# A two-layer hybrid decoder trunk on one core: the mix chunks spilled from the gate tile through another queue, the weight preparation tied to matmuls, and the second GLA norm emitted inside the first convolution

## The chip, the cores and the metric

The kernel runs on one core of one Trainium2 chip. Its time is the device time of one execution in microseconds (us); the figure quoted is the median of several runs. The engines are named as the profile names them: PE is TensorE (matmuls; PEld are its weight loads), DVE is VectorE, ACT is ScalarE, POOL is GpSimd and SP is SyncE. Each engine works through its own instructions in order. DMAs are issued by an engine's queue: SP's (SPq), ACT's (ACTq) or POOL's (POOLq).

## What is computed

There are two layers over 512 tokens of width 2048 in float32. A layer normalises its input and projects it with one wide matrix. The result feeds three branches, which are joined, projected once more and added to the input:

```python
def _layer(x, norm_g, w_in, conv_w, conv_b, sb_qn_g, sb_kn_g, gla_w_up, gla_b_up, gla_on_g, w_out):
    h = _rmsnorm(x, norm_g)
    cv_h, cv_b, cv_c, cv_g, sb_q, sb_k, sb_v, sb_g, gl_q, gl_k, gl_v, gl_g, gl_lr = split(h @ w_in)
    y_conv = _short_conv(cv_h, cv_b, cv_c, conv_w, conv_b) * silu(cv_g)      # causal, width 3
    y_sb = _stick_breaking(rms(sb_q), rms(sb_k), sb_v) * silu(sb_g)          # 8 heads of 128
    g = log_sigmoid(gl_lr @ gla_w_up + gla_b_up) / 16
    o = _gla(gl_q, gl_k, gl_v, g)                                            # 4 heads, state of 64 x 128
    y_gla = _rmsnorm(o, gla_on_g) * silu(gl_g)
    return x + concatenate([y_conv, y_sb, y_gla], axis=-1) @ w_out
```

So each of the three branches is 512, 1024 and 512 columns of the joined "mix" of 2048 columns, and each is multiplied by a gate of its own.

## The kernel before

**Weights.** Both weight matrices are streamed in groups of 256 columns; a list (`specs`) gives their order. In a layer the groups are: GLA v 0 and v 1 (v 1 with the low-rank columns), GLA q, GLA k, GLA gate 0 and 1, convolution h, c, g, b (half 0), then four times v, g, q, k of the attention, convolution h, c, g, b (half 1), and eight groups of the output matrix. A matmul works in float16 and keeps float32 accuracy by splitting each operand into a high and a low part, with three matmuls for each product. Preparing group i is this chain:

- `fetch` (L359): two DMAs of 1 MB into the staging tile "st", of which there are two. All but the first three groups are issued by POOL.
- `wmax` (L370): a square with an accumulated maximum or sum on ACT, one for each of the two halves of the tile. `wscale` takes the sum over partitions (POOL `partition_all_reduce`, L383) and forms the scale with small DVE instructions.
- then `whi` (ACT, L436) and `wlo` (DVE, L444) write the high and low parts of each half. For the groups called "quick" (the attention's g and k, the convolution's h of half 1, and three or four output groups of a layer) `wsums` writes seven combinations instead (ACT L476, DVE L477, and the accumulating copy L494 on POOL), so that the projection takes seven products rather than eight.

`weights()` is called by each projection for its group i: it starts the fetch of i + 2 and, before this change, `load(i + 1)`: squares, scale and parts of the next group, with high priority and the squares held behind the first high part of group i (`anchor`). The order of the engines' instructions is decided by a scheduler from the order of emission, the dependencies, and these holds (`order` is a dependency without a semaphore's data).

**Projections.** `project_cols` (L663 to L673 are its three matmuls and those of `project_toks`), `project_quick` (L750 and L753) and `project_by_token` (L797) multiply the input's parts with a group's parts into PSUM banks "psp" (three buffers). The quick products are combined by evictions on ACT (L761, L765, L768) and DVE (L763), and TensorE reuses a bank only after its eviction.

**GLA.** The two halves p = 0, 1 run one after the other. For each the level matrices are built (L995 to L1090), the final products (L1090, 48 matmuls) accumulate the half's outputs in PSUM, and for each of two heads hh the norm follows: o times a scale (DVE), its square (ACT L1098), a matmul by `avg` into "psm" (L1100), logarithm and exponential (ACT L1102, L1103), DVE steps L1104 to L1109, of which the last multiplies by the gate `gg[p]`, and `mixsplit`.

**The mix.** `mixsplit` makes the high (ACT L857) and low (DVE L858) parts of one 128-column chunk of the mix in a tile "ga" (two buffers, 128 x 2 x 512 float16) and spills it to DRAM (`mixd`, 256 KB) with a DMA from SP (L860), 24 times in all. The gate tiles have tag "g", two buffers too. `project_gate` (L822 to L829) evicts a gate's projection with ACT (L822) into a "g" tile, then computes its SiLU with four ACT instructions into a "ga" tile (L824 to L826, L828). At half 1 of the convolution `mixload` reads the chunks back.

**Where the stages stand.** The norm of p = 0 runs at the end of convolution half 0, about when its gate is evicted (the first layer's last part of it ends at 237.29 us). The norm of p = 1 is emitted after its final products, ahead of convolution h. In the order of the scheduler these products stand inside the projection of the attention's v 0, and the norm's two matmuls L1100 behind it, ahead of the accumulating products of g 0.

Of the kernel before, what the change touches and what calls it, by code (L numbers as in the profile page):

```python
# [43 lines left out]
def hybrid_trunk(ctx, tc, x, norm_g, w_in, conv_w, conv_b, sb_qn_g, sb_kn_g,  # L44
# [294 lines left out]
    def load(i):  # L339
        with tc.high_priority():  # L340
            load_(i)

# [23 lines left out]
    def wmax(i, h):  # L366

        if h == 0:
            peak[i] = sm(2 + (i in narrow), "wm")
        S.activation(junk(HK * GW).rearrange("p (k n) -> p k n", k=HK), staged[i][h], AF.Square,  # L370
                     accum_out=peak[i][:, h:h + 1])
        if h and i in narrow:
            S.activation(junk(KT * LR).rearrange("p (k n) -> p k n", k=KT), narrow[i], AF.Square,
                         accum_out=peak[i][:, 2:3])

    def wscale(i):
# [4 lines left out]
        if i:  # L381
# [4 lines left out]
            V.tensor_tensor(m, gm[:, 0:1], gm[:, 1:2], ALU.add)  # L386
        else:

            ps = bank(psm, "m")[:, :1]
            pk = peak.pop(i)  # L390
            for j, (a, b) in enumerate(((ones, pk[:, 0:1]), (ones, pk[:, 1:2]), (pk[:, 2:3], pk[:, 2:3]))):
                T.matmul(ps, a.to_broadcast([P, P]), b, start=j == 0, stop=j == 2)
# [10 lines left out]
        scales[i] = sc  # L403

# [26 lines left out]
    anchor = {}  # L431

    def whi(i, h):
# [3 lines left out]
        anchor.setdefault(i, hi)  # L437
# [23 lines left out]

    def wsums(i):
# [18 lines left out]
        if specs[i][1] is w_out:  # L481
# [6 lines left out]
            anchor[i] = split(b12, 2)  # L488
# [7 lines left out]
        anchor[i] = split(b22, 3)  # L496
# [9 lines left out]
    def weights():  # L506
# [140 lines left out]
    for l in range(depth):  # L647
# [3 lines left out]
        def project_cols():  # L651
# [3 lines left out]
            for h in range(2):  # L655
                wh, wl = w[h]
                for c, o in enumerate(ps):
                    cs = slice(c * P, (c + 1) * P)
                    for kk in range(HK):
# [5 lines left out]
                        T.matmul(o, wl[:, kk, cs], xh[:, :, k, :], start=False, stop=en)  # L665
            return ps, u

        def tok_mm(o, ah, al, w, t, k, n, st_, en):
# [4 lines left out]
            T.matmul(o, al[:, t, k, :], wh[:, kk, :n], start=False, stop=en, skip_group_check=True)  # L673

        def project_toks(ah, al, late=()):
# [59 lines left out]
        def project_quick(src, sums, y, cols):  # L735
# [7 lines left out]
            def prod(o, w, a, start, stop=False):  # L743
                for t in range(1 if cols else 2):
                    for kk in range(HK):
                        for i, (p_, q_) in enumerate(((0, 0), (0, 1), (1, 0))):
                            st_ = start and t == kk == i == 0
                            en = stop and kk == HK - 1 and i == 2
                            if cols:
                                T.matmul(o, w[q_][:, kk, :], a[p_][:, :, kk, :], start=st_, stop=en,  # L750
                                         skip_group_check=True)
                            else:
                                T.matmul(o[:, t * P:(t + 1) * P], a[p_][:, t, kk, :], w[q_][:, kk, :], start=st_,  # L753
                                         stop=en, skip_group_check=True)
# [653 lines left out]
```

## Time and profile before

| | us |
|---|---|
| median of 3 runs | 1780.85 |
| lowest, highest | 1779.24, 1786.48 |
| the profiled execution | 1789.68 |
| its span, first to last instruction | 1787.5 |

The granted TensorE clock over the span is 0.981 of full. Busy times in the span: PE 1685.7 us (94%), DVE 1340.1 (75%), ACT 1131.2 (63%), POOL 218.2 (12%). The DMA engines moved 227.25 MB.

A line of the profile gives the line of the kernel, the engine and the operation with its tiles (output, then inputs). A bracket behind an instruction is the time in which its engine stood idle before it and what ended that.

### The profile page before, as it was taken

To read this page: it belongs to the slowest core of one execution; us is meant where nothing else is said; L and a number is where in the kernel's file an instruction comes from. 1 tells how busy PE (TensorE), PEld (TensorE's weight loads), DVE (VectorE), ACT (ScalarE), POOL (GpSimd) and SP (SyncE) were. 2 spreads that over 40 slices of the span, in tenths; PEclk is the share of its full clock that TensorE was granted. 3 is DMA by queue.
4 is the path that set the end of the run, shared out by engine and by line. 5 is a ranking of instruction groups with operands and counts; after the bars stand their busy time and mean duration, and the time that the engine had idled before them with its cause. 6 is when DMAs were issued, how large, how long until landed. Compare 5 with 4: busy or idle time off the path is not lost.

```text
span 1787.5 us, 36869 instructions
## 1 busy us (share of the span) xinstructions
PE 1685.7 (94%) x15642; PEld 1306.6 (73%) x15642; DVE 1340.1 (75%) x2327; ACT 1131.2 (63%) x1619; POOL 218.2 (12%) x262
## 2 busy tenths in 40 slices
PE   7999995999999999999989999959999899999999
PEld 5644554888989884689976454649888888748898
DVE  8966887577777787686688577866777777768874
ACT  7667664576666676566665675556676666755652
POOL 1210110011111111011111101001111111100100
PEclk9999998999999999999999999989999999999999
DMA  7233341357656867355544233224576677763441
GB/s 241 92 98 95 95 118 55 76 131 136 143 136 143 143 166 206 77 163 169 192 98 142 90 100 106 60 59 111 110 170 103 138 134 165 223 150 102 158 144 49
DMA packets 204517, 227.25 MB, mean 127 GB/s; under 512 B 118770, under 2 KB 166204, under 8 KB 203840
## 3 DMA queue, kind: packets, MB, share of 16 engines
q0 software_dynamic: 58432, 162.54, 32.6%
q1 hardware_dynamic: 136912, 52.90, 14.4%
q10 hardware_dynamic: 9008, 9.45, 1.6%
q8 instruction: 122, 2.00, 0.5%
q14 instruction: 43, 0.35, 0.1%
HBM read 179.65 MB, written 14.68 MB: 109 GB/s over the span
## 4 chain that ended last, share of the span: by engine, by line
PE 19%; DVE 13%; DMA 12%; ACT 7%; issue 3%; POOL 1%; POOLq 0%; ACTq 0%; DVEq 0%
DMA st<-in_w_in_dram 5%; PE psp L753 5%; ACT junk L370 3%; DMA st<-in_w_out_dram 3%; PE psp L797 3%; DVE wl L477 3%; DMA qT<-qp 2%; PE psp L673 2%; PE psp L750 2%; PE psp L671 2%; PE psp L672 2%; PE psp L664 1%; PE psp L663 1%; PE psp L665 1%; DVE wl L444 1%
## 5 line engine op out<-in xcount | busy, mean ns | idle before, releaser
L370 ACT ACTIVATE junk<-st 128x2048 uint8<-128x2048 f32 x150 | 285.8, 1905 | 129.6 <-DMA st<-in_w_in_dram 94.9
L444 DVE SCALAR_TENSOR_TENSOR wl<-st,ws,wh 128x2048 f16<-128x2048 f32 x102 | 239.2, 2346 | 51.6 <-ACT wh L436 51.1
L671 PE MATMUL psp<-wh,m 128*128 128x256 f16 x960 | 261.8, 273 | 1.6 <-ACT m L1127 1.6
L672 PE MATMUL psp<-wl,m 128*128 128x256 f16 x960 | 261.8, 273 | 0.0
L673 PE MATMUL psp<-wh,m 128*128 128x256 f16 x960 | 261.8, 273 | 0.0
L436 ACT ACTIVATE wh<-st,ws 128x2048 f16<-128x2048 f32 x100 | 199.1, 1996 | 68.0 <-PE psp L664 32.2
L477 DVE SCALAR_TENSOR_TENSOR wl<-st,ws,wh 128x1024 f16<-128x1024 f32 x150 | 189.4, 1278 | 35.7 <-ACT wh L476 35.6
L476 ACT ACTIVATE wh<-st,ws 128x1024 f16<-128x1024 f32 x150 | 165.6, 1139 | 64.5 <-PE psp L673 33.6
L359 POOL DMA_DIRECT2D st<-in_w_in_dram x114 | 103.7, 926 | 476.9 <-DVE wl L444 219.8
L673 PE MATMUL psp<-wh,x 128*128 128x256 f16 x512 | 139.7, 273 | 0.0
L672 PE MATMUL psp<-wl,x 128*128 128x256 f16 x512 | 139.6, 273 | 0.0
L671 PE MATMUL psp<-wh,x 128*128 128x256 f16 x512 | 139.5, 273 | 0.0
L383 POOL PARTITION_ALL_REDUCE wgm<-wm x75 | 38.1, 508 | 811.1 <-ACT junk L370 797.7
L665 PE MATMUL psp<-x,wl 128*128 128x512 f16 x352 | 134.1, 381 | 2.2 <-DVE wl L444 2.2
L750 PE MATMUL psp<-s,wh 128*128 128x256 f16 x640 | 113.8, 279 | 23.6 <-ACT g L761 21.4
L663 PE MATMUL psp<-x,wh 128*128 128x512 f16 x352 | 134.2, 381 | 0.0
L664 PE MATMUL psp<-x,wh 128*128 128x512 f16 x352 | 133.9, 381 | 0.0
L663 PE MATMUL psp<-m,wh 128*128 128x512 f16 x352 | 133.4, 379 | 0.0
L664 PE MATMUL psp<-m,wh 128*128 128x512 f16 x352 | 133.4, 379 | 0.0
L665 PE MATMUL psp<-m,wl 128*128 128x512 f16 x352 | 133.2, 379 | 0.0
L665 PEld LDWEIGHTS <-wl 128*128 128x128 f16 x704 | 69.0, 98 | 83.2 <-DVE wl L444 2.7
L663 PEld LDWEIGHTS <-wh 128*128 128x128 f16 x704 | 69.0, 98 | 81.4 <-issue 1.7
(426 smaller groups left out, 4001.5 us busy)
## 6 DMA issues: line engine op xcount, KB each, us to landing
st<-in_w_in_dram POOLq DMA_DIRECT2D x114, 1024.0 KB, 8.3
st<-in_w_out_dram POOLq DMA_DIRECT2D x32, 1024.0 KB, 7.6
st<-st POOLq DMA_DIRECT2D x18, 512.0 KB, 9.5
st<-in_w_in_dram SPq DMA_DIRECT2D x6, 1024.0 KB, 11.8
mixd<-ga SPq DMA_DIRECT2D x24, 256.0 KB, 10.0
x<-in_x_dram SPq DMA_DIRECT2D x4, 1024.0 KB, 4.9
qT<-in_x_dram ACTq DMA_DIRECT2D x8, 512.0 KB, 4.7
qT<-xs ACTq DMA_DIRECT2D x8, 512.0 KB, 4.1
```

The costliest lines, as they stand in the source:

```text
L370: S.activation(junk(HK * GW).rearrange("p (k n) -> p k n", k=HK), staged[i][h], AF.Square, accum_out=peak[i][:, h:h + 1])
L436: hi = S.activation(wh[:, :, :GW], staged[i][h], AF.Copy, scale=scales[i])
L444: V.scalar_tensor_tensor(wl[:, :, :GW], staged[i][h], scales[i], wh[:, :, :GW], ALU.mult, ALU.subtract)
L476: hi = S.activation(h_, b, AF.Copy, scale=sc)
L477: V.scalar_tensor_tensor(l_, b, sc, h_, ALU.mult, ALU.subtract)
L663: T.matmul(o, wh[:, kk, cs], xh[:, :, k, :], start=st_, stop=False)
L664: T.matmul(o, wh[:, kk, cs], xl[:, :, k, :], start=False, stop=False)
L665: T.matmul(o, wl[:, kk, cs], xh[:, :, k, :], start=False, stop=en)
L671: T.matmul(o, ah[:, t, k, :], wh[:, kk, :n], start=st_, stop=False, skip_group_check=True)
L672: T.matmul(o, ah[:, t, k, :], wl[:, kk, :n], start=False, stop=False, skip_group_check=True)
L673: T.matmul(o, al[:, t, k, :], wh[:, kk, :n], start=False, stop=en, skip_group_check=True)
L750: T.matmul(o, w[q_][:, kk, :], a[p_][:, :, kk, :], start=st_, stop=en, skip_group_check=True)
```

## The change

There are five edits.

1. `mixsplit` gets the dead half of the gate tile (the half whose gate has just been multiplied in) and writes both parts of the chunk into it, as float16 in the space of 512 float32 numbers a partition. No "ga" tile is taken for this. The spill is issued by POOL instead of SP.
2. `load` and `anchor` are gone. `weights()` leaves two closures in `hooks`; the projection that uses group i calls `hook(mm)` at two of its matmuls. The first hook emits the squares of group i + 1 and orders the first square behind that matmul (the first triple of the projection), the second emits the scale and the parts and orders the first instruction of the scale behind its matmul, which stands about a quarter into the projection. In `project_quick` these are the first triple of the first product and the last matmul of the second product.
3. The norm of GLA's half p becomes a closure for each hh. The first half's are called at once, as before. The second half's are kept and called from the two `then()` points of `conv_in(0)`: after the eviction of convolution h's projection, and after the convolution.
4. `insums = xsums()` (the combined parts of the input for the quick products) is emitted after the loop over GLA's q and k instead of before.
5. The callers of `mixsplit` pass the dead gate half.

The core of the diff:

```diff
-    def load(i):
-        with tc.high_priority():
-            load_(i)
...
 def wmax(i, h):
...
-        S.activation(junk(HK * GW).rearrange("p (k n) -> p k n", k=HK), staged[i][h], AF.Square,
-                     accum_out=peak[i][:, h:h + 1])
+        sq = S.activation(junk(HK * GW).rearrange("p (k n) -> p k n", k=HK), staged[i][h], AF.Square,
+                          accum_out=peak[i][:, h:h + 1])
...
+        return sq
...
 def wscale(i):
...
+        first = V.tensor_tensor(m, gm[:, 0:1], gm[:, 1:2], ALU.add)
...
+        return first
...
-    anchor = {}
+    hooks = []
...
-    def load_(i):
-
-        with tc.issue_after(anchor[i - 1].ins):
-            for h in range(2):
-                wmax(i, h)
-        wscale(i)
-        if i in quick:
-            wsums(i)
-            return
-        for h in range(2):
-            whi(i, h)
-            wlo(i, h)
+    def squares(i, mm):
+
+        with tc.high_priority():
+            for h in range(2):
+                a = wmax(i, h)
+                if not h:
+                    order(a, mm)
+
+    def parts_of(i, mm):
+
+        with tc.high_priority():
+            order(wscale(i), mm)
+            if i in quick:
+                wsums(i)
+                return
+            for h in range(2):
+                whi(i, h)
+                wlo(i, h)
+
+    def hook(mm):
+
+        if hooks:
+            hooks.pop(0)(mm)
...
 def weights():
...
+        assert not hooks
         if i and i + 1 < len(specs):
-            load(i + 1)
+            hooks.extend([lambda mm: squares(i + 1, mm), lambda mm: parts_of(i + 1, mm)])
         return loaded.pop(i)
...
 def project_cols():
...
+                        if not h and not c and kk in (0, HK - 1):
+                            hook(mm)
...
 def project_toks(ah, al, late=()):
...
-                        tok_mm(o, ah, al, w, t, k, GW, k == 0 and t % 2 == 0, k == lastk)
+                        mm = tok_mm(o, ah, al, w, t, k, GW, k == 0 and t % 2 == 0, k == lastk)
+                        if not t and k == 0 or t == 1 and k == rounds[0][-1]:
+                            hook(mm)
...
 def project_quick(src, sums, y, cols):
...
+                            if start and t == kk == 0 and i == 2 and o is pa:
+                                hook(mm)
+                return mm
...
-            prod(pb, wT2, s_, True)
+            hook(prod(pb, wT2, s_, True))
...
 def project_by_token(ah, al, n):
...
+                        if not t and (not i and not k or i == 2 and k == KT - 1):
+                            hook(mm)
...
-        def mixsplit(k, y, s_):
+        def mixsplit(k, y, s_, dead):
...
-                hl = wk([P, 2, NT, P], "ga", dt=F16)
+                hl = dead.bitcast(F16).rearrange("p (i t c) -> p i t c", i=2, t=NT)
...
-                nc.sync.dma_start(mixd[l][:, :, k, :], hl.rearrange("p i t c -> p (i t) c"))
+                nc.gpsimd.dma_start(mixd[l][:, :, k, :], hl.rearrange("p i t c -> p (i t) c"))
...
-        insums = xsums()
         scr = [wk([P, 2, 2, seq], *a, F16) for a in (("qp", 1), ("th", 2), ("th", 2))]
...
+        insums = xsums()
         gq, gk = qk
...
-        gg, gsc = [], []
+        gg, gsc, norms = [], [], []
...
-            for hh in range(2):
+            def norm(hh, p=p, ops2=ops2):
+
                 ops_ = ops2[:, hh, :]
...
-                mixsplit(12 + 2 * p + hh, o_, gsc[p])
+                mixsplit(12 + 2 * p + hh, o_, gsc[p], gg[p][:, hh, :])
+
+            norms.extend([lambda f=norm: f(0), lambda f=norm: f(1)])
+            while not p and norms:
+                norms.pop(0)()
...
-                mixsplit(2 * j + c, y[:, c, :], s_)
-
-        conv_out(0, conv_in(0))
+                mixsplit(2 * j + c, y[:, c, :], s_, g[:, c, :])
+
+        conv_out(0, conv_in(0, lambda: norms.pop(0)()))
...
-                mixsplit(4 + 2 * j + hh, y.rearrange("p t c -> p (t c)"), s_)
+                mixsplit(4 + 2 * j + hh, y.rearrange("p t c -> p (t c)"), s_, g[:, hh, :])
```

More of the change, by code (lines that the diff above doesn't have):

```diff
@@ L390, in wscale @@
             pk = peak.pop(i)
+            first = None
             for j, (a, b) in enumerate(((ones, pk[:, 0:1]), (ones, pk[:, 1:2]), (pk[:, 2:3], pk[:, 2:3]))):
@@ L487, in wsums @@
             split(b22, 1)
-            anchor[i] = split(b12, 2)
+            split(b12, 2)
             V.tensor_tensor(b22, b22, b21, ALU.add)
@@ L495, in wsums @@
         split(b11, 0)
-        anchor[i] = split(b22, 3)
+        split(b22, 3)
         V.tensor_tensor(b22, b12, b22, ALU.add)
@@ L672, in tok_mm @@
             T.matmul(o, ah[:, t, k, :], wl[:, kk, :n], start=False, stop=False, skip_group_check=True)
-            T.matmul(o, al[:, t, k, :], wh[:, kk, :n], start=False, stop=en, skip_group_check=True)
+            return T.matmul(o, al[:, t, k, :], wh[:, kk, :n], start=False, stop=en, skip_group_check=True)
         def project_toks(ah, al, late=()):
@@ L796, in project_by_token @@
                     for k in range(KT):
-                        T.matmul(o[:, :n], a_[:, t, k, :], w[k // HK][part][:, k % HK, :n],
-                                 start=i == 0 and k == 0, stop=i == 2 and k == KT - 1)
+                        mm = T.matmul(o[:, :n], a_[:, t, k, :], w[k // HK][part][:, k % HK, :n],
+                                      start=i == 0 and k == 0, stop=i == 2 and k == KT - 1)
+                        if not t and (not i and not k or i == 2 and k == KT - 1):
+                            hook(mm)
                 ps.append(o)
```

12 lines of the change are left out of this document (5 added, 7 removed).

## The prediction

> **What bounds the kernel now.** I read the page's head and slices first. Columns of the long row are busy time, mean of one, then idle time before it and what ended most of that.
>
> ```profile
> span 1787.5 us, 36869 instructions
> ...
> PE 1685.7 (94%) x15642; PEld 1306.6 (73%) x15642; DVE 1340.1 (75%) x2327; ACT 1131.2 (63%) x1619; POOL 218.2 (12%) x262
> ...
> PE   7999995999999999999989999959999899999999
> ...
> PEclk9999998999999999999999999989999999999999
> ...
> L370 ACT ACTIVATE junk<-st 128x2048 uint8<-128x2048 f32 x150 | 285.8, 1905 | 129.6 <-DMA st<-in_w_in_dram 94.9
> ```
>
> TensorE (PE) is busy 1685.7 of 1787.5 us, so the most that any reordering can win is the 102 us in which it is not, plus the time in which the clock was granted low. The slices show two dips, in both layers at the same place (the 59s), and ACT's squares of the incoming weights (L370), which wait 94.9 us for weight DMAs: the weight supply runs close to demand. The next view is what TensorE waited for (total us, times, longest).
>
> ```profile
> PE psp L750 <- ACT g L761: 21.4, 2, 10.8
> PE psp L750 <- ACT g L768: 14.4, 8, 3.1
> PE psm L1100 <- ACT e L1098: 14.2, 2, 7.1
> ...
> PE psp L753 <- ACT kT L768: 4.2, 2, 3.0
> ```
>
> Three waits are 21.4, 14.4 and 14.2 us. Two of them happen once per layer (10.8 and 7.1 us) and are the dips. The timeline of the first dip names the chain; the bracket is the idle time of that engine just before the instruction, and what ended it.
>
> ```profile
> 298.34 2.07 PE L1100 MATMUL psm<-e,avg 128*128 128x512 f32 x2 [7.09 <-ACT e L1098]
> ...
> 303.82 6.08 SPq L860 DMA_DIRECT2D mixd<-ga  x2
> ...
> 308.61 0.75 DVE L858 SCALAR_TENSOR_TENSOR ga<-za,gsmix,ga 128x512 f16<-128x512 f32 x1 [0.79 <-ACT ga L857]
> 313.64 0.63 ACT L824 ACTIVATE ga<-g 128x512 f32<-128x512 f32 x1 [5.06 <-DMA mixd<-ga]
> 314.18 0.36 ACT L761 ACTIVATE g<-psp 128x256 f32<-128x256 f32 x1
> ...
> 314.59 0.37 PE L750 MATMUL psp<-s,wh 128*128 128x256 f16 x1 [10.79 <-ACT g L761]
> ```
>
> The second half's GLA norm stands in this place. Its matmul L1100 is in TensorE's queue ahead of the quick products of the first attention gate (g0), and waits 7.09 us for ACT L1098. Then L858 ends at 309.36, its spill through SP is in flight, and ACT L824, which writes a "ga" tile, sits 5.06 us because both "ga" buffers are held by spills. ACT is in order, so the eviction L761 behind it comes at 314.18, and TensorE resumes after 10.79 us. Both dips are thus a queue order and a buffer, not work. The stretches below give what they are worth (from:to and length in us; busy us and instructions of PE, PEld, DVE, ACT, POOL; granted clock; DMA share; GB/s).
>
> ```profile
> 225.00:250.00 25.00, 25.00 (x133) 12.05 (x132) 19.61 (x36) 18.81 (x26) 3.80 (x4) 1.00 0.46 120
> 285.00:335.00 50.00, 30.46 (x227) 23.79 (x225) 32.84 (x47) 28.19 (x37) 2.18 (x3) 0.83 0.22 64
> 1163.00:1212.00 49.00, 29.71 (x219) 23.10 (x217) 32.78 (x47) 27.57 (x37) 2.18 (x3) 0.83 0.22 65
> 298.34:303.80 5.46, 5.46 (x26) 3.42 (x27) 5.42 (x8) 2.85 (x4) 0.37 (x1) 0.68 0.00 0
> 314.59:319.47 4.88, 4.88 (x24) 3.34 (x24) 1.39 (x2) 3.27 (x6) 0.00 (x0) 0.56 0.00 0
> 398.00:424.50 26.50, 24.46 (x205) 20.28 (x204) 20.76 (x29) 16.75 (x19) 4.68 (x6) 0.94 0.63 112
> 577.00:603.00 26.00, 23.49 (x211) 20.09 (x209) 19.24 (x25) 16.75 (x19) 3.91 (x5) 1.00 0.59 110
> 1459.00:1486.00 27.00, 24.91 (x209) 20.81 (x208) 21.76 (x29) 18.76 (x23) 4.11 (x6) 0.94 0.49 137
> 1687.70:1752.30 64.60, 60.24 (x1056) 59.27 (x1056) 52.54 (x70) 39.37 (x45) 6.53 (x9) 1.00 0.44 142
> ```
>
> In 285 to 335 TensorE idles 50.00 - 30.46 = 19.5 us, in 1163 to 1212 it idles 49.00 - 29.71 = 19.3. After the two waits it restarts slowly: 5.46 us at clock 0.68 and 4.88 at 0.56, which loses 5.46 x 0.32 + 4.88 x 0.44 = 3.9 us. A layer's dip costs about 23.4 us, both 46.8.
>
> **The change part by part.**
>
> *Norm deferred, spill out of the "ga" tile.* The norm of the second half is 2 matmuls (L1100), 8 ACT and 16 DVE instructions per layer; none is added or dropped. By the instruction order of the two programs, the second half's 48 final products and both L1100 now stand between the quick products of g0, with 11 or more products between one part of the norm and the next, and hi/lo no longer takes a "ga" tile, so L824 has no spill to wait for. Both named waits lose their cause: 46.8 us. What is late next is DVE: it is busy 32.84 us of the 50, and the stretch shrinks to about 29 us, so some 4 us of its work (the end of the norm) has to run on beside the next projection; I keep back 2 us per layer as new short waits. Saving 46.8 - 4 = 43.
>
> *Parts of weights behind matmuls.* The instructions are the same (150 squares), only held to a place in TensorE's stream. Where it matters is the seventh product of the attention's gates:
>
> ```profile
> 417.87 1.91 ACT L370 ACTIVATE junk<-st 128x2048 uint8<-128x2048 f32 x1 [4.11 <-DMA st<-in_w_in_dram]
> ...
> 419.78 0.36 ACT L768 ACTIVATE g<-psp 128x256 f32<-128x256 f32 x1
> ```
>
> L768 is the eviction that TensorE waits for. It stands on ACT behind a square that itself waited 4.11 us for the weight. ACT's order stays the same here in the changed program, but TensorE now has 24 matmuls of the next projection ahead of the seventh product instead of 8. The 398 to 424.5 stretch gives 24.46/205 = 0.119 us a matmul, so 16 more cover 1.9 us. The eight waits are 1.8 us on average and 3.1 at most, so I take 11 of the 14.4 as saved. Clock 0.94 in the stretches at 398 and 1459 loses 0.06 x 53.5 = 3.2 us there; this goes with the waits. The attention's k groups lose cover instead, from 18 matmuls to none in some (18 x 0.119 = 2.1 us): bounds 0 and three times 2.1 per layer, so 0 to 13; I take 3, the L753 row's 4.2 us being the nearest. Together -11.
>
> The Trainium skill (TensorE: Matmul & The Clock Gate, section "What's actually happening") says that the clock drops after about 3.4 us idle, in a free-running window. The row speaks otherwise in part: a wait of about 2 us was followed by 0.94 in two stretches, and 577 to 603 with its similar wait stayed at 1.00. By the rule the 3.2 us would be 0; the sum goes by the rows.
>
> *Layer 1's output groups.* Here the weight loop sets the time:
>
> ```profile
> 1710.51 1.78 POOL L359 DMA_DIRECT2D st<-in_w_out_dram  x2 [8.46 <-DVE w7l L477]
> ...
> 1731.93 1.78 POOL L359 DMA_DIRECT2D st<-in_w_out_dram  x2 [8.45 <-DVE w7l L477]
> ```
>
> ```profile
> 1720.91 1.91 ACT L370 ACTIVATE junk<-st 128x2048 uint8<-128x2048 f32 x1 [1.85 <-DMA st<-in_w_out_dram]
> ...
> 1728.61 1.15 ACT L476 ACTIVATE w7h<-st,ws 128x1024 f16<-128x1024 f32 x1 [2.32 <-DVE st L489]
> ```
>
> From one fetch issue to the next is 21.42 us, and TensorE's work for a group is 60.24/3 = 20.08 (the 1687 stretch holds three). The loop is fetch, second square at 1720.91 (10.4 us after the issue), then the splits on ACT, of which w7h comes last at 1728.61, 5.8 us after the square's end. In the changed order the second square stands behind the earlier weight's splits and w7h follows it sooner, so the loop drops below 20 us, and TensorE bounds: (21.42 - 20.08) x 4 groups = 5.4. I take 5.
>
> *Spills on POOL.* 24 spills move.
>
> ```profile
> st<-in_w_in_dram POOLq DMA_DIRECT2D x114, 1024.0 KB, 8.3
> ...
> st<-st POOLq DMA_DIRECT2D x18, 512.0 KB, 9.5
> ...
> mixd<-ga SPq DMA_DIRECT2D x24, 256.0 KB, 10.0
> ```
>
> ```profile
> L359 POOL DMA_DIRECT2D st<-in_w_in_dram x114: 882/899/1592, 59.0 to 1546.6; - x114
> ```
>
> ```profile
> L494 POOL DMA_DIRECT2D st<-st x18: 1578/1600/1621, 245.3 to 1501.9; - x18
> ```
>
> ```profile
> L860 SPq DMA_DIRECT2D mixd<-ga x24: 512/514/613, 230.0 to 1540.6; - x24
> ```
>
> On SP an issue takes 0.514 us. On POOL no spill was seen; between the nearest rows, a weight's issue of 0.899 and the accumulating copy's of 1.600, 24 spills keep POOL busy for 22 to 38 us, of a span in which POOL has 12% work. That hides unless a fetch or a reduce that is due stands behind a spill that waits for DVE L858. Bounds: nothing, or 24 x 1.6 = 38 us plus the waits. I take 3, since by the program order most spills stand where POOL idles as it does ahead of the two issues above (8.45 us). SP loses the spills; nothing there was waited for except the two 5 us above, so that gives nothing more.
>
> *Dead gate tile.* The spill now holds a "g" tile, of which there are two, so the next gate's eviction waits for it. The tight one is the first convolution's gate after the first half's norm:
>
> ```profile
> 236.55 0.74 DVE L858 SCALAR_TENSOR_TENSOR ga<-za,gsmix,ga 128x512 f16<-128x512 f32 x1
> ```
>
> ```profile
> 235.95 0.67 ACT L822 ACTIVATE g<-psp,wu 128x512 f32<-128x512 f32 x1
> 236.52 1.99 ACT L436 ACTIVATE wh<-st,ws 128x2048 f16<-128x2048 f32 x1
> ...
> 240.83 0.67 ACT L822 ACTIVATE g<-psp,wu 128x512 f32<-128x512 f32 x1
> ```
>
> L858 ends at 237.29; with an issue of 0.9 to 1.6 and a landing 8.3 to 10.0 later, the tile would be free at 246 to 249, while L822 ran at 235.95 and 240.83. In the changed order L858 stands a few us earlier and L822 behind it, and TensorE has work in hand (it is busy 25.00 of 25.00 us from 225 to 250, where both evictions lie), 10 us of it by my estimate from the order of its products. Bounds: 0, or the whole 246 - 236 = 10 to 13 us per layer; I take 2 per layer, 4 in all. The other reuses come a whole projection later, and a group's 20.08 us of matmuls cover an issue and a landing of under 12; I cost them nothing. If the cover is gone, the weight split L436 queued behind L822 is late too.
>
> *The rest.* Moving the sums of the input's parts (insums) is hidden by TensorE's full stretch at 225. At the start of the output projection the hold puts squares and splits of the first output group behind a matmul of the last convolution: 0 to 5 us per layer by one weight's two squares and a split (2 x 1.9 + 2.0 = 5.8 on ACT, some of it idle there); I take 2 per layer, 4 in all. Weights are prepared later everywhere: 0 to 10, by the 94.9 us of waits on L370 that may reach TensorE; I take 2.
>
> **Sum.** -43 - 11 - 5 + 3 + 4 + 4 + 2 = -46 us. It is made against the profiled execution, 1789.68 us (its span is 1787.5), which stands 8.8 above the median 1780.85; the same -46 on the median gives **1735 us**.
>
> **The rivals.**
>
> 1. *The spill's wait moves to L822* (two buffers of "g" in place of two of "ga"). For it: the landing of 8.3 to 10.0 us above, and that L822 follows L858 at once. Against: TensorE has work in hand. If the wait is paid in full, 11 us idle plus 4 us of low clock per layer (as after the waits of 7.1 and 10.8) in place of 2: -46 + 26 = -20, so 1761. Chance 0.14.
> 2. *The norm's wait stays, only later*: L1100 waits for the DVE chain inside g0's products too. Then 14.2 us and about 3.5 of low clock return: -28, so 1753. For it: DVE's 32.84 of 50. Against: 11 or more products between the steps. Chance 0.08.
> 3. *POOL's queue, slower.* A spill on POOL waits for L858 and holds the fetch (L359) or the reduce (L383) behind it, and the weight chain, whose squares already waited 94.9 us for DMAs, hands it on to TensorE. It eats the whole gain from 46/24 = 1.9 us per spill. At 2.8 us per spill, 1.6 of issue and 1.2 of standing, it costs 67: +21, so 1802. Against: L359's slowest issue is 1.59 us, so 0.7 over its median, and POOL idles 88%. Chance 0.11. The Trainium skill (SBUF — State Buffer, section "SBUF: two separate sides") warns that a DMA issued by POOL has its descriptors held up while VectorE runs certain two-port operations, and advises SP or ACT; by it this rival would come true. The trace agrees at most weakly, with 882/899/1592 ns for 114 issues beside a DVE that is 75% busy.
> 4. *All named gaps go at no price*: 46.8 + 14.4 + 3.2 + 5.4 = 70, so 1711. Against: DVE and ACT in the dips are 60% busy. Chance 0.10.
>
> **How the numbers follow.** The forecast as worked out has 0.57, with its own range 1722 to 1750. A change of 0.5% (8.9 us) is about what a measurement of this kernel tells from none. Cases 1, 2, 4 and the forecast are faster, 0.89, of which 0.05 lies within 0.5% (case 1 with more waits behind L822): faster 0.84, same 0.05, slower 0.11. The range holds the forecast, 1, 2 and 4, and their uncertain costs: 1710 to 1765. Left out is case 3 and the edges.
>
> **What would show it.** In the changed profile, the waits L750 <- L761 and L1100 <- L1098 should be gone or under 1 us each, the clock of the dips near 1.0, and the time between the end of v0 and the end of g0 shorter by 20 us. L768's waits should be under 1.5 us each. The fetch interval in layer 1's output groups should be 20 us. The spills should show as POOL issues, of 0.9 to 1.6 us, with no fetch late behind them. An ACT L822 waiting over 5 us on a DMA of mixd shows rival 1; a wait of L1100 inside g0's products rival 2; longer idle times of L383 or L370 behind spills, with TensorE waiting for weight parts (L436, L444, L476, L477), rival 3. The prediction is wrong if TensorE's total idle does not fall by over 30 us.

## The result

The changed kernel takes 1713.26 us (median of 3 runs, 1713.0 to 1717.69) against 1780.85: 67.6 us less, ratio 0.9621 with a 95% interval of 0.958 to 0.9662. The forecast was 1735, so the sign and the range held and the gain is half as large again as forecast. The profiled execution took 1717.69 us, 4.4 above the median, with a span of 1715.9 against 1787.5, so the spans differ by 71.6 us.

Line numbers shift by the diff: L359 became L355, L370 L366, L750 L764, L753 L767, L761 L778, L768 L785, L822 L841, L824 L843, L857 L876, L858 L877, L860 L879, L1100 L1119, L1203 L1226. The head of the page of the changed kernel, and the row of the squares:

```profile
span 1715.9 us, 36876 instructions
...
PE 1669.9 (97%) x15642; PEld 1298.4 (76%) x15642; DVE 1331.3 (78%) x2327; ACT 1129.1 (66%) x1619; POOL 239.2 (14%) x286
...
PE   7999999999999989999989999999999999899999
...
PEclk9999999999999999999999999999999999999999
...
L366 ACT ACTIVATE junk<-st 128x2048 uint8<-128x2048 f32 x150 | 285.1, 1901 | 44.1 <-DMA st<-in_w_in_dram 42.8
```

TensorE's idle time (the span less 1685.7 then, less 1669.9 now) fell from 102 to 46 us, and its busy time by 15.8 us for the same 15642 matmuls: that part goes with the clock, which was granted at 0.981 of full and is now at 0.992. Both 59 dips are gone from the slices. The squares wait 42.8 us for weights, no longer 94.9: the weight supply has more room, not less. What TensorE waits for most is something that the profile of before did not have:

```profile
PE psz L1226 <- DMA kT<-qp: 11.0, 2, 5.9
PE psp L764 <- ACT g L785: 5.5, 6, 1.9
```

The first row is a new wait, for the transposed keys. L785 is the old seventh product's wait, which was 14.4 us in eight. The two waits of the dips (L764 for L778's eviction of g, and L1119: 10.8 and 7.1 us, once per layer) are gone. The stretches of the changed kernel, cut at the last matmul of the named groups, show where the rest went. The columns are those of the prediction's view of stretches, and in both layers the stretches are v 0 and g 0; q 0 and k 0; v 1 to k 3; the second convolution; the output groups.

```profile
core 0: us, PE busy (x) PEld busy (x) DVE busy (x) ACT busy (x) POOL busy (x), PEclk, DMA share, GB/s
258.13:307.31 49.18, 49.18 (x475) 42.86 (x474) 46.21 (x83) 37.00 (x63) 8.71 (x10) 1.00 0.42 114
307.31:346.49 39.18, 39.18 (x526) 37.07 (x524) 31.75 (x58) 29.16 (x55) 8.09 (x9) 1.00 0.52 132
346.49:605.62 259.13, 257.13 (x2845) 233.56 (x2844) 207.11 (x372) 176.90 (x277) 42.20 (x46) 1.00 0.66 144
605.62:700.62 95.00, 88.48 (x502) 48.80 (x499) 65.28 (x117) 61.28 (x75) 10.35 (x15) 0.96 0.61 161
700.62:865.40 164.78, 163.21 (x1989) 151.84 (x1987) 120.88 (x157) 103.19 (x151) 18.28 (x25) 1.00 0.51 161
1101.27:1151.03 49.76, 49.47 (x475) 42.79 (x474) 46.79 (x85) 37.78 (x64) 9.05 (x10) 1.00 0.42 116
1151.03:1190.21 39.18, 39.18 (x526) 37.05 (x524) 31.85 (x58) 28.84 (x54) 7.71 (x8) 1.00 0.52 134
1190.21:1458.15 267.94, 259.32 (x2845) 235.06 (x2844) 207.35 (x372) 177.12 (x277) 41.47 (x46) 0.99 0.71 139
1458.15:1551.63 93.48, 87.42 (x502) 48.46 (x499) 64.50 (x115) 58.42 (x70) 11.85 (x16) 0.98 0.64 165
1551.63:1712.60 160.97, 160.97 (x2131) 151.57 (x2128) 119.44 (x144) 81.82 (x84) 12.34 (x17) 1.00 0.37 124
```

Against the same stretches of before:

| stage | before, layer 0 and 1 | after | difference |
|---|---|---|---|
| up to the first convolution's end | 259.73, 236.30 | 258.13, 235.87 | -2.0 |
| v 0 and g 0 | 74.98, 74.80 | 49.18, 49.76 | -50.8 |
| q 0 and k 0 | 44.60, 48.57 | 39.18, 39.18 | -14.8 |
| v 1 to k 3 | 266.79, 266.95 | 259.13, 267.94 | -6.7 |
| second convolution | 87.59, 87.69 | 95.00, 93.48 | +13.2 |
| output groups | 166.98, 169.17 | 164.78, 160.97 | -10.4 |

They add up to -71.5. Two cautions belong to the small rows. In q 0 and k 0 some 5 us of the 14.8 is work that now lies in the neighbouring rows: 18 matmuls of v 1 that stood ahead of k 0's last product and 5 of q 0 that now stand ahead of g 0's, at 0.11 us each in both layers. And single profiles differ: in that of `b_defer` (below), whose time is that of before, v 1 to k 3 takes 263.66 and 264.09 us, so the -6.7 of that row is no more than two profiles of equally fast kernels differ by.

In the stretch of v 0 and g 0 TensorE is now busy 49.18 of 49.18 us at clock 1.00. The same stretch of before:

```profile
259.73:334.71 74.98, 53.54 (x470) 44.04 (x469) 52.15 (x86) 40.31 (x68) 2.18 (x3) 0.89 0.15 43
```

There it idled 21.4 us at clock 0.89. In one row time is lost: in the second convolution 13.2 us are given back.

### The profile page after: what moved, and what is told of

Read it like the earlier page. It is cut to its first block, busy times and chain, and to the rows that moved or that the text cites. A ratio compares the mean times of both kernels' runs of the same rounds, so it can differ in the third digit from the quotient of the medians.

```text
span 1715.9 us, 36876 instructions
## 1 busy us (share of the span) xinstructions
PE 1669.9 (97%) x15642; PEld 1298.4 (76%) x15642; DVE 1331.3 (78%) x2327; ACT 1129.1 (66%) x1619; POOL 239.2 (14%) x286
## 3 DMA queue, kind: packets, MB, share of 16 engines
q1 hardware_dynamic: 111952, 46.61, 14.4%
## 4 chain that ended last, share of the span: by engine, by line
PE 73%; DVE 12%; DMA 7%; ACT 4%; issue 3%; POOL 0%; DVEq 0%; ACTq 0%
PE psp L767 13%; PE psp L674 8%; PE psp L675 8%; PE psp L673 8%; PE psp L685 7%; PE psp L684 7%; PE psp L683 7%; PE psp L814 6%; PE psp L764 3%; DMA st<-in_w_in_dram 2%; DVE wl L486 2%; DMA th<-za 2%; DMA kT<-qp 2%; ACT junk L366 1%; DVE wl L442 1%
## 5 line engine op out<-in xcount | busy, mean ns | idle before, releaser
L366 ACT ACTIVATE junk<-st 128x2048 uint8<-128x2048 f32 x150 | 285.1, 1901 | 44.1 <-DMA st<-in_w_in_dram 42.8
L435 ACT ACTIVATE wh<-st,ws 128x2048 f16<-128x2048 f32 x100 | 199.3, 1998 | 105.4 <-PE psp L674 47.1
L355 POOL DMA_DIRECT2D st<-in_w_in_dram x114 | 102.2, 900 | 436.0 <-DVE wl L442 319.4
L673 PEld LDWEIGHTS <-wh 128*128 128x128 f16 x704 | 69.2, 98 | 81.5 <-issue 3.1
L674 PEld LDWEIGHTS <-wh 128*128 128x128 f16 x704 | 69.2, 98 | 80.8 <-issue 2.3
```

Of the source, the lines that this page charges most:

```text
L366: sq = S.activation(junk(HK * GW).rearrange("p (k n) -> p k n", k=HK), staged[i][h], AF.Square, accum_out=peak[i][:, h:h + 1])
L435: hi = S.activation(wh[:, :, :GW], staged[i][h], AF.Copy, scale=scales[i])
L673: T.matmul(o, wh[:, kk, cs], xh[:, :, k, :], start=st_, stop=False)
L674: T.matmul(o, wh[:, kk, cs], xl[:, :, k, :], start=False, stop=False)
```

## The experiments

Each theory is named in the expectations: theory 1 is that the tile which `mixsplit` writes is what the dips were made of, theory 2 that the new wait is TensorE's order alone, theory 2b that the transposes are slow because of the reads ahead of them, theory 3 that of the two hooks it is the squares' that counts. The rival of the first is the prediction's own step, which gave the dips to the deferred norm and the spill together.

**One part alone.** `b_spill` is the kernel before with the dead gate tile and POOL's queue:

```diff
-                hl = wk([P, 2, NT, P], "ga", dt=F16)
+                hl = dead.bitcast(F16).rearrange("p (i t c) -> p i t c", i=2, t=NT)
...
-                nc.sync.dma_start(mixd[l][:, :, k, :], hl.rearrange("p i t c -> p (i t) c"))
+                nc.gpsimd.dma_start(mixd[l][:, :, k, :], hl.rearrange("p i t c -> p (i t) c"))
```

> The kernel before with the spill edit alone: the chunk's parts go into the dead gate tile and POOL issues the spill; weights are still loaded behind the anchor, the norm of the second half is not deferred, the sums of the input stand where they stood. Theory 1: this edit alone empties the dips of v0 and g0 (by its order the norm's matmuls L1100 stand in q0's projection and no ga tile is held), so 1780.85 - 47 = 1733 us, and the new wait for kT at the second convolution is there or not independent of it. Rival (the prediction's step, which gave the dips to the deferral and the spill together): the 7.1 us waits of the norm's matmul stay, so only 2 x (10.8 + 2) go and it gives 1755 us.

Measured: 1733.26 us, ratio 0.9725 (0.9688 to 0.9761). The stretch of v 0 and g 0 in this kernel:

```profile
260.28:309.41 49.13, 47.75 (x467) 41.85 (x466) 44.60 (x77) 29.91 (x51) 8.19 (x9) 1.00 0.32 96
```

It takes 49.13 us of the 74.98, so this one edit empties the dip. The norm's matmul (here L1138), which is not deferred, doesn't bring the 7.1 us back: it now stands behind g 0, in q 0's projection, and waits 1.4 us.

```profile
311.38 1.12 PE L1138 MATMUL psm<-e,avg 128*128 128x512 f32 x2 [1.43 <-ACT e L1136]
```

What the edit leaves is the seventh product's wait:

```profile
PE psp L783 <- ACT g L804: 14.7, 6, 3.2
...
PE psz L1245 <- DMA kT<-qp: 4.1, 2, 2.1
```

14.7 us, as before: the spill doesn't touch it. The wait for kT (here L1245) is already there, with 4.1 us.

`b_defer` is the kernel before with the norm of the second half in closures, called at the two `then()` points:

```diff
-            for hh in range(2):
+            def norm(hh, p=p, ops2=ops2):
...
-        conv_out(0, conv_in(0))
+        conv_out(0, conv_in(0, lambda: norms.pop(0)()))
```

> The kernel before with the deferred second norm alone. Theory 1: deferral moves nothing that counts (by the instruction order L1100 stands where it stood): 1781 us, within 5. Rival (the prediction's step): the 7.1 us wait per layer goes, and its low clock: 1780.85 - 14.2 - 3.5 = 1763 us.

Measured: 1783.24 us, ratio 0.9998 (0.9983 to 1.0013). No gain at all. `a_no_defer` asks the reverse, the changed kernel with `while norms:` in place of `while not p and norms:`:

> The changed kernel with the second half's norm emitted at once, as before. Theory 1: the same time, 1713 us within 4, as TensorE's order is the same. Rival: the norm's matmul waits in g0 again: 1713.3 + 14.2 + 3.5 = 1731 us.

Measured: 1716.59 us, ratio 0.9627 (0.9596 to 0.9658), beside the changed kernel's 0.9621. Neither added nor taken away does the deferral move the time by more than the intervals; that the deferral ends the 7.1 us waits is refuted twice.

`b_hooks` is the kernel before with `squares`, `parts_of` and the hooks in place of `load` and `anchor`:

```diff
-        if i and i + 1 < len(specs):
-            load(i + 1)
+        if i and i + 1 < len(specs):
+            hooks.extend([lambda mm: squares(i + 1, mm), lambda mm: parts_of(i + 1, mm)])
```

> The kernel before with the hooks alone (squares and parts of the next weight behind matmuls), spill from a ga tile through SP and norm at once as before. Theory 1: the dip's 10.8 us wait (ACT held by two ga tiles) stays in both layers, while the seventh-product waits, k0 and layer 1's output groups gain: 1780.85 - 15 (q0, k0) - 7 (attention) - 9 (output groups) + 0 to 13 (wait for kT) = 1750 to 1763 us. Rival: the hooks also undo the dips, by making room on ACT: 1720 us.

Measured: 1762.48 us, ratio 0.9877 (0.9837 to 0.9917), inside theory 1's 1750 to 1763, at its upper end. What TensorE waited for most there:

```profile
PE psp L764 <- ACT g L778: 9.5, 2, 5.2
PE psp L764 <- DVE v L1287: 8.7, 2, 4.4
PE psp L764 <- ACT g L785: 8.2, 8, 2.1
PE psz L1226 <- DMA kT<-qp: 7.3, 2, 4.0
```

Two waits of 5 us for L778 and two of 4 for DVE L1287 stand in the dips, whose stretch takes 66.83 us: the hooks shorten the dips by 8 us a layer and don't remove them. The seventh product's waits (L785) fell to 8.2 us, and the wait for kT is 7.3. Against the 1782.35 us that the kernel before took beside these runs, the spill alone gives 49.1 and the hooks alone 19.9, in sum 69.0; together they gave 67.6. The medians add up, but not stage by stage: the 8 us a layer that the hooks take off the dip are among those that the spill takes off it too, since the dip's stretch is 49 us with the spill alone and with both.

**Tile or queue.** `a_ga_tile` is the changed kernel with the parts in a "ga" tile again, spilled by POOL (the line `hl = wk([P, 2, NT, P], "ga", dt=F16)`):

> The changed kernel with the chunk's parts in a ga tile again, spilled by POOL. Theory 1: the tile is what the dips were made of, so ACT L843 waits for spills again and about 20 us a layer come back, less what the other order saves: 1745 us, 1735 to 1755. Rival: the queue was what counted (SP's spill landed late), so 1713 us within 6.

Measured: 1755.04 us, ratio 0.9847 (0.9804 to 0.9889), at theory 1's upper bound. The dip's stretch is back at 66.82 us:

```profile
259.06:325.88 66.82, 52.81 (x470) 43.83 (x468) 50.42 (x85) 39.89 (x67) 7.89 (x9) 0.92 0.27 66
```

The expectation had a wrong picture of how. It said that L843 would wait for spills; here is ACT in that dip:

```profile
304.20 0.72 ACT L876 ACTIVATE ga<-za,gsmix 128x512 f16<-128x512 f32 x1 [3.35 <-DVE za L1128]
304.83 0.61 ACT L843 ACTIVATE ga<-g 128x512 f32<-128x512 f32 x1
305.35 0.36 ACT L778 ACTIVATE g<-psp 128x256 f32<-128x256 f32 x1
```

L843, the gate's SiLU that takes a "ga" tile, waits for no DMA. It stands right behind L876 of the norm's last chunk, which had waited 3.35 us for the norm's last DVE step, and the eviction L778 that TensorE needs stands behind L843. So with the tile shared the cost is that the gate is put behind the norm's whole chain. The landing of the spill, 5.06 us in the profile of before, came on top there. The order of TensorE shows it too. In each of the four kernels that write the chunk into a "ga" tile (before, `b_defer`, `b_hooks`, `a_ga_tile`) the norm's matmuls stand ahead of all 168 products of g 0, in both layers; where the dead gate tile is used they stand among them (behind 72 and 166 in the changed kernel) or behind all 168 (`b_spill`, `b_dead_sp`). That the order goes with the tile is shown; that the turn of the two buffers is what forces it is argued.

`a_spill_sp` is the changed kernel with `nc.sync.dma_start` for the spill, and `b_dead_sp` the same for `b_spill`:

> The changed kernel with the spills issued by SP instead of POOL; they are still written from the dead gate tile. Theory 1: the queue gives nothing, the tile does: 1713 us within 6. Rival 3 of the prediction (spills on POOL hold up the weights): faster, 1705 us or less. Another rival: SP's transposes of q, k and the attention weights stand behind the spills again and TensorE's wait for kT grows: 1720 us or more.

> The kernel before with the dead gate tile alone: the parts go there, SP still issues the spill. Theory 1: the tile carries the gain of the spill edit and the queue only a few us, as in the changed kernel, where spills on SP cost 9: 1733 + 5 = 1738 us, within 6. Rival: without the hooks SP's queue matters more or POOL's order carries the dips: 1750 us or more.

Measured: 1722.86 us, 0.9657 (0.9627 to 0.9687), and 1736.71 us, 0.9743 (0.9718 to 0.9767). `b_dead_sp` came as theory 1 had it. `a_spill_sp` lies outside theory 1's 1713 within 6 and in the time of the last rival (1720 us or more), but not by that rival's mechanism: TensorE's wait for kT did not grow, it is 7.2 us against 11.0, and in `b_dead_sp` there is none. Both runs are a little slower than with POOL (1713.26 and 1733.26), by 6 and 3 us when the ratios are compared, and both intervals overlap those of the twin: a gain from POOL's queue is not shown, nor a loss. The first row and the landing are the changed kernel's, then those of `a_spill_sp`:

```profile
L879 POOL DMA_DIRECT2D mixd<-g x24: 851/907/1615, 223.2 to 1470.6; - x24
```

```profile
mixd<-g POOLq DMA_DIRECT2D x24, 256.0 KB, 7.7
```

```profile
L879 SPq DMA_DIRECT2D mixd<-g x24: 512/513/619, 222.8 to 1477.1; - x24
...
DMA to landing us min/median/max: 2.8/5.7/11.4
```

POOL's issue takes 0.907 us and its spill lands after a median of 7.7 us; SP's takes 0.513 and 5.7. In the pair without the hooks it is the other way round, 7.8 us with POOL (`b_spill`) and 10.2 with SP (`b_dead_sp`), so neither queue lands sooner in general. Rival 3's first half is in the trace of the changed kernel: POOL stood idle ahead of eight spills, 68.6 us in all, of which 51.0 for DVE L877. Its second half is not: TensorE's waits for weight parts did not grow, 10.2 us before and at most 7.7 now.

**What of the hooks.** `a_parts_free` holds only the squares:

```diff
-            order(wscale(i), mm)
+            wscale(i)
...
-            hooks.extend([lambda mm: squares(i + 1, mm), lambda mm: parts_of(i + 1, mm)])
+            hooks.extend([lambda mm: (squares(i + 1, mm), parts_of(i + 1, mm)), lambda mm: None])
```

> The changed kernel with the squares of the next weight held behind the first matmul triple, but its scale and parts emitted at the same place and not held behind a matmul. Theory 3: what the hooks bring is the squares' place (they no longer stand ahead of evictions and splits on ACT), so the time stays near 1713 us, 1710 to 1719. Rival: holding the parts is what counts: the 20 us between the spill alone (1733) and the changed kernel mostly come back, 1725 us or more.

Measured: 1716.43 us, ratio 0.9625 (0.9611 to 0.964). Holding the parts is worth nothing that can be measured. What the hooks bring is the hold of the squares, or the place inside the projection at which both are emitted; this run doesn't separate the two. The output groups of layer 1 take 160.97 us in it as in the changed kernel.

`a_insums_early` puts `insums = xsums()` back ahead of the loop over q and k:

> The changed kernel with the sums of the input emitted ahead of the loop over GLA's q and k, as before. Theory 1: TensorE is full in those stages and nothing waits for the sums until g0: 1713 us within 4. Rival: the sums crowd DVE and ACT during q and k, and gq or the gates' levels come late: 1718 us or more.

Measured: 1715.59 us, ratio 0.9624 (0.961 to 0.9638). That edit moves nothing.

**The new wait.** In the changed kernel's second convolution, SP's queue and TensorE show:

```profile
617.17 7.09 SPq L887 DMA_DIRECT2D m<-mixd  x4
625.02 13.34 SPq L1341 DMA_TRANSPOSE kT<-qp  x2
638.53 1.01 SPq L887 DMA_DIRECT2D m<-mixd  x2
```

```profile
633.90 0.38 PE L675 MATMUL psp<-x,wl 128*128 128x512 f16 x1
640.15 0.69 PE L1226 MATMUL psz<-kT,qT 128*128 128x512 f16 x2 [5.87 <-DMA kT<-qp]
640.63 0.63 PE L673 MATMUL psp<-x,wh 128*128 128x512 f16 x1
```

SP issues four reads of the mix, then the two transposes of kT, which take 13.34 us to issue, of which the first 8.40, and then two more reads. TensorE reaches the first scores (L1226) after 633.90 + 0.38 and waits 5.87 us; the matmuls behind it then go at half pace (one every 0.43 us, where there had been one every 0.22), at a granted clock of 0.50 for 5 us:

```profile
640.15:645.15 5.00, 5.00 (x13) 1.83 (x13) 0.00 (x0) 0.86 (x1) 0.00 (x0) 0.50 0.97 329
```

The second layer repeats it with 5.2 us. In the kernel before, SP had these reads and transposes too, with five reads straight ahead of the transposes, and TensorE didn't wait:

```profile
659.87 12.69 SPq L868 DMA_DIRECT2D m<-mixd  x5
672.66 9.07 SPq L1318 DMA_TRANSPOSE kT<-qp  x2
```

```profile
683.94 0.43 PE L1203 MATMUL psz<-kT,qT 128*128 128x512 f16 x2
```

The difference is the place of these scores in TensorE's order. Before, 81 matmuls of the convolution's c stand ahead of them, and in the changed kernel 43. The other runs follow: 81 in `b_dead_sp`, without a wait, 48 in `b_spill` (4.1 us), 47 in `b_hooks` (7.3) and in `a_spill_sp` (7.2).

`a_scores_mid` calls the first scores of the last group from inside the projection of the convolution's c, ordered behind its 72nd matmul:

```diff
-            then()
-            uc = wk([P, 2, seq], "raw", 1) if j else wk([P, 2, seq], "zw")
-            ps, u = project(True, lambda: uc)
+            if not j:
+                then()
+            uc = wk([P, 2, seq], "raw", 1) if j else wk([P, 2, seq], "zw")
+            ps, u = project(True, lambda: uc, (lambda mm: then(mm)) if j else None)
...
+                        if mid and h and not c and kk == HK - 1:
+                            mid(mm)
```

> The changed kernel with the first scores of the last attention group put 72 matmuls into the second convolution's c projection instead of 43, so that TensorE works while the transposes of kT land. Theory 2 (the new wait of 5.9 and 5.2 us is TensorE's order alone, and costs 11.0 us idle and some 4 of low clock): 1713.3 - 13 = 1700 us. Rival: the group's later end holds up the first output group, which reads its chunks last, so that the gain is given back: 1710 us or more.

Measured: 1702.6 us, ratio 0.955 (0.9514 to 0.9586). The wait is down from 11.0 us to

```profile
PE psz L1229 <- DMA kT<-qp: 2.0, 3, 1.2
```

and the second convolution takes 86.88 and 88.26 us, where the changed kernel took 95.00 and 93.48. The 13.3 us of this stage come back as 10.7 in the time. Nothing later is held up: the output groups take 164.78 and 160.97, as in the changed kernel.

`a_loads_behind` leaves the scores and orders the six reads behind the transposes (`order(d, turned[-1])` for each read `d`):

> The changed kernel with all six reads of the mix ordered behind the last transposes of kT on SP; in the changed kernel four of them stand ahead. Theory 2b (the transposes are slow, 8.4 us for the first, because the reads lie ahead of them in SP's ring): the first takes about 5 us, the wait for kT shrinks from 5.9 to 2 or 3 us, so 1706 us. Rival: they are slow because of the weight's fetch on the same DMA engines: 1713 us within 4, the wait as it was.

Measured: 1712.58 us, ratio 0.9603 (0.957 to 0.9637). SP's queue and the wait:

```profile
626.19 5.98 SPq L1342 DMA_TRANSPOSE kT<-qp  x2
632.34 4.14 SPq L887 DMA_DIRECT2D m<-mixd  x6
```

```profile
PE psz L1227 <- DMA kT<-qp: 6.4, 2, 3.3
```

```profile
634.86 0.43 PE L1227 MATMUL psz<-kT,qT 128*128 128x512 f16 x2 [3.03 <-DMA kT<-qp]
```

Without the reads ahead of them the two transposes take 5.98 us to issue instead of 13.34, and the wait falls from 11.0 to 6.4 us, 3.2 each. So moving the reads does make the transposes faster, as theory 2b said. The wait understates the gain, because with this edit the scores moved too: only 28 matmuls of c stand ahead of them here. Counted from the start of the stretch, the scores began 6.2 us sooner than in the changed kernel (28.35 against 34.53), which is the whole of the wait of 5.87, but TensorE also reached them 3.3 us sooner. In the second layer they began 5.1 us sooner, against a wait of 5.2. The second convolution is 5.5 and 1.8 us shorter in the profiled execution (89.53 and 91.64 us). In the medians the 7 us expected didn't show: the difference is 0.7, the rival's number, and the two intervals overlap. Whether the reads slow the transposes by lying ahead of them in the queue or by their bytes on the same DMA engines, the run doesn't separate.

`a_scores_mid_lb` is both:

> The changed kernel with both: the last group's scores later in the second convolution, and the reads of the mix behind the transposes of kT. Theory 2: the scores alone removed all but 2.0 us of the wait, so the reads add 0 to 2: 1701 us within 4. Rival: the reads come so much later that the output projection waits for the mix: 1708 us or more.

Measured: 1700.94 us, ratio 0.9536 (0.9514 to 0.9558). The interval lies below the changed kernel's (0.958 to 0.9662), so this version beats both kernels, by some 12 and 83 us. It is not apart from `a_scores_mid`.

## Why the prediction was right, and where not

**Right in sign and in the main mechanism, too small in size.** The chain of waits read from the profile of before (the norm's chunk, the "ga" tile, L824, L761) was the thing that went. The share that the forecast gave to the deferred norm was wrong. It kept back costs that hardly came, and missed one that did.

1. *Norm deferred, spill out of the "ga" tile: -43 forecast, -50.8 measured in v 0 and g 0.* Half of the step's cause is wrong: the tile alone brings the gain (`b_spill`, `b_dead_sp`, `a_ga_tile`). The deferral, to which the step gave the 7.1 us waits, is worth nothing alone (ratio 0.9998) and costs nothing when undone (1716.59). And the 4 us kept back for DVE were not there: TensorE is busy 49.18 of 49.18, with DVE at 46.21. The named price, 46.8 us, was itself a little low: with v 0 the idle time is 21.4 us a layer, and the quoted stretch had 19.5.
2. *Parts of weights behind matmuls: -11 forecast, -21.5 measured in q 0 to k 3, not all of it by the hooks.* Alone the hooks took 12.9 us off this stretch (`b_hooks`: 43.51 and 40.33 us for q 0 and k 0, 261.87 and 268.32 for v 1 to k 3), and the spill 4.5. So the forecast of 11 is near what the hooks did alone; the rest is beside the caution on single profiles above. The seventh product's waits fell from 14.4 to 5.5 us, so 8.9 of the 11 came, by the mechanism given: ACT's order is the same, TensorE has more matmuls in hand. With the spill alone they stay at 14.7, which shows that the hooks do it. No wait was longer than 1.9 us, where I expected under 1.5. The term for the k groups had the wrong sign: I charged 3 us, and q 0 and k 0 gained 9.3 with the hooks alone, some 4 of it by matmuls of v 1 that moved out of the stretch. The hold of the parts, which I had taken for a piece of it, does nothing (`a_parts_free`).
3. *Layer 1's output groups: -5 forecast, -8.2 measured.* The mechanism was right, the term mis-sized. From fetch to fetch it is now

```profile
1641.56 1.78 POOL L355 DMA_DIRECT2D st<-in_w_out_dram  x2 [2.08 <-DVE wq L392]
...
1660.47 1.79 POOL L355 DMA_DIRECT2D st<-in_w_out_dram  x2 [2.09 <-DVE wq L392]
```

18.91 us, not the 20.08 that I took for TensorE's work. That figure came of a miscount: the stretch from 1687.7 has 1056 matmuls and a group 336, so it holds 3.14 groups and not three. 60.24/3.14 is 19.2 us, and TensorE without a wait needs 18.9. The hooks bring this gain: `b_hooks` takes 161.08 us there. Of the 8.2, some 2 may be the profile's, since `b_defer` took 167.16 and not 169.17.
4. *Spills on POOL: +3 forecast, no cost measured clear of noise.* The Trainium skill's warning about DMAs issued by POOL (SBUF — State Buffer, section "SBUF: two separate sides") isn't borne out by the time of this case. With a DVE that is 78% busy, the 24 issues took 851 to 1615 ns, and landed 2.0 us later than SP's in the changed kernel (7.7 against 5.7) but 2.4 sooner in the pair without hooks. Which DVE instructions are of the kind that it means, no trace here shows.
5. *The gate's wait for the spill: +4 forecast, nothing for TensorE measured.* The wait is there, and the timeline has it:

```profile
234.59 0.85 POOL L879 DMA_DIRECT2D mixd<-g  x1 [4.61 <-DVE g L877]
```

```profile
238.40 1.27 ACT L841 ACTIVATE g<-psp,wu 128x512 f32<-128x512 f32 x2 [0.71 <-DMA mixd<-g]
```

L841 waited 0.71 us, and 1.28 in the second layer. The spill issued at 234.59 had landed by 238.4, so in 3.8 us and not in the 8.3 to 10.0 that I took; TensorE idled nowhere in that projection. Rival 1 is refuted with it.
6. *The output projection's start +4, later weights +2: 0 measured.* The first output group got 1.8 us shorter in layer 0 and the same in layer 1, and the squares wait 52 us less for their weights. With the hooks alone the cost is there in one layer: `b_hooks` takes 29.2 us for layer 0's first output group, against 24.4 before, with a wait of 2.8 us for a high part (ACT L435).
7. *Not foreseen: the second convolution, +13.2.* The prediction went through what each edit moves on ACT, POOL and at the dips, and took the edits of SP's queue for harmless ("that gives nothing more"). But the scheduler also put the last group's scores earlier in TensorE's order, behind 43 matmuls of c in place of 81, and so ahead of where kT lands. `a_scores_mid` shows that their place is enough to cause the wait, and by `a_loads_behind`, where kT was there 6.2 and 5.1 us sooner, faster transposes would have covered it as well. Two of the edits bring the scores forward, the hooks (47 matmuls, 7.3 us) and the spill on POOL (48, 4.1 us); the dead gate tile with SP's queue doesn't (`b_dead_sp`: 81, no wait). With all of them it is 11.0 us.

The terms kept back (13 us, and the 4 in step 1) and the missed loss of 13 nearly cancel; what remains is the underrated gains. That the time lies in the range is in part luck: the lower bound was 1710, and without the loss that I missed the time is 1702.6 (`a_scores_mid`). Rival 4, with 1711 us, came nearest, though by another sum than its own: named gaps at no price, less 13, plus gains that it didn't name. It had 0.10, which looks too little now: six allowances, the 3 us for the k groups among them, were unknowns that could have been zero, and I charged something for every one.

What stays open is a difference of 7.7 us between profiles of one layer's attention: layer 1's v 1 to k 3 took 267.94 us in the changed kernel and 260.27 in `a_no_defer`, whose program differs there by nothing that TensorE's order shows. Two waits of TensorE stand in the first profile and not in the second, 3.55 us of L1263 for DVE L1270 and 1.41 of L1226 for ACT L1236. What brings them is not traced. What the 20 us of the hooks are made of is open too, between the hold of the squares and the place where they are emitted.

## What to carry to other kernels

When a short-lived tile shares its buffers with another stage's, look at who has to come behind whom, not only at how long the DMA holds the buffer: a dead tile at hand may cost nothing and let a chain float. Undo each edit by itself before giving it a share of the gain: here one that looked like half of the cause moved nothing. Count the matmuls of a stretch before dividing by its groups, and do not charge every unknown. After a change that lets TensorE run ahead, look for the next transfer that it now meets too early; here its scores met the transposes, and moving them by 29 matmuls gave 10.7 us more.

## What the runs showed of the hardware

The issue of a DMA transpose on SP had no fixed length: in the changed kernel the 16 of kT took 1.23 to 8.40 us. The longest stood behind reads of the mix (two took 13.34 us in the changed kernel), and with the reads behind them the same two took 5.98. The reads are not all of it, since in `a_spill_sp` the first, behind four reads, took 5.60 us, and the second, behind six, 2.03. A spill of 256 KB landed after a median of 7.7 us from POOL's queue and 5.7 from SP's in the changed kernel, 7.8 and 10.2 without the hooks. And TensorE's granted clock was 0.50 over the 5 us behind the wait of 5.87 us for kT, which makes such a wait cost more than it shows.
